# Two of the six selection blocks of a sparse-attention layer move from the attention heads into the indexer

## The chip, the core and the metric

The kernel runs on one core of a Trainium2 chip. The metric is the time of one execution on the device in microseconds (us), the median of three runs. The core has a matrix engine (PE, with weight loads as PEld), a vector engine (DVE), an activation engine (ACT), a general engine (POOL) and DMA queues fed by SP. Each engine takes its instructions strictly in the order of its own queue and waits at an instruction until the semaphores that it names are there.

## The reference, cut to what matters

The program is a decoder trunk of two layers (sequence 1024, width 1024). Layer 0 has two groups of softmax heads, layer 1 has eight stick-breaking heads and eight sparse heads, and each layer ends in a gated MLP with a short convolution. Only layer 1's attention is touched. Its sparse heads see, for each query, the 256 keys that an indexer scores highest:

```python
logits = jnp.einsum('bqhd,bkd->bqhk', iqb, ik)                 # 4 index heads of 64, one shared key
score = jnp.einsum('bqhk,bqh->bqk', jax.nn.relu(logits), iwb)  # weighted sum over the index heads
score = jnp.where(kpos[None, None, :] <= qpos[None, :, None], score, -jnp.inf)
_, sel = lax.top_k(score, top_k)                               # top_k = 256
```

```python
def stick_breaking_attention(q, k, v):
    z = einsum('bqhd,bkhd->bhqk', qb, k) * scale
    log1m = where(kpos < qpos, log_sigmoid(-z), 0)
    after = cumsum(log1m, reverse=True) - log1m
    a = where(kpos < qpos, exp(log_sigmoid(z) + after), 0)     # in the kernel: sigmoid, running product, multiply
    return einsum('bhqk,bkhd->bqhd', a, v)
```

## The kernel before, in words

Everything runs in fp32 as products of high and low halves: a product is three matmuls (`three`), and an operand is split by ACT (the high half) and DVE (the low half, L190). Queries go in eight blocks of 128. Block i sees 128 x (i+1) keys, so its score row is 128(i+1) wide. The order in each engine's queue is set by a scheduler from the order in which the program emits work, so emission acts as a priority; a PE instruction that is emitted early stands early in PE's queue.

The layer's attention has two stages.

**The index** (`index`, from L920). For each of eight token tiles of 128 it makes a key tile (a projection of 24 matmuls, 256 wide, in `proj_tok` with the weights `uk`; ACT's copy out at L929; a rotation on POOL, a norm) and a query tile (the same with `uq`). `keys(half)` transposes four key tiles (L913) and splits them; `scored(half, xs, b)` transposes the query tiles of one half for two index heads, and then for each block of that half and each head does the score matmuls (`psS<-kh,qs`), a relu on ACT (L978) and an update of the block's score tile `sc[i]` on DVE (L979). The two first blocks, 0 and 1, have at most 256 keys and need no selection, so `sc` exists for blocks 2 to 7. Before, the order is: key tiles 0 to 3, `keys(0)`, key tiles 4 to 7, query tiles (with `keys(1)` and the first scores among them), then the rest of the scores. Beside it runs `fill`, which takes units from a list of other projections (`between`): q and k of the first pair of heads (weights `w1t`), then 16 tiles of v (weights `w1v`).

Weights come through `wunit`: a raw load into `ra` (two buffers in all), a copy of the high half on ACT (`hx` for the index's weights, `ha` for the others, L200) and the low half on DVE (`lx`, `la`). `hx` and `lx` have two buffers each, just enough for `uk`, or for `uq`. A weight unit thus needs a free `ra`, and its copy needs a free `hx`.

**The heads.** Eight stick-breaking heads, then eight sparse heads. For each block a stick-breaking head does: scores on PE into `psS` (two buffers), two sigmoids on ACT (L758, L759), a running product on DVE (L761), a multiply on POOL (L763), transposes of the result and the product with v on PE, with copies on ACT (L355) and DVE (L190 `ptl`) between.

**The selection** (`topk`, L1003) finds, per query, the value of the 256th highest score by bisection over the 32 bits. It runs as a list of steps beside the heads: `next(todo)` after each block above 2, five per head. One round counts, for every block, how many scores reach the candidate: on DVE (L1025, one pass over the row with a sum) for the blocks in `by_dve`, on ACT (a Sign with a sum, L1032) for those in `by_act`; then DVE sets the next candidate for all blocks at once with three operations on a tile of 128 x 6 (L1051 `tkY`, L1052 `tkC`, L1047 `tkG`). The round's counts need the candidate, and the next candidate needs all counts. After 32 rounds come one count for each ACT block (greater than), and for each block a finishing of five passes on DVE (L1025, L1069, L1071, L1072, L1073) and one on POOL (L1074), which turn `sc[i]` into a mask. Before, `by_dve, by_act = [5, 6], [2, 3, 4, 7]`: all six blocks in one search. Its first round stands ahead of head 0, rounds 2 to 31 stand in heads 0 to 5, and round 32 with the finishing in heads 6 and 7. The sparse heads need the masks.

Of the kernel before, what the change touches and what calls it, by code (L numbers as in the profile page):

```python
# [10 lines left out]
F32 = mybir.dt.float32  # L11
# [3 lines left out]
I8 = mybir.dt.int8  # L15
U32 = mybir.dt.uint32
# [6 lines left out]
P = 128  # L23
D = 1024
S = 1024
NT = S // P
# [29 lines left out]
class Net:  # L56
# [660 lines left out]
    def odd_attn(self, h):  # L717
        nc, tc, A = self.nc, self.tc, self.A
        unit = partial(self.wunit, lo_eng="vector")
        with ExitStack() as st:  # L720
            ep = st.enter_context
            kv = ep(tc.tile_pool(name="kv", bufs=1))
            iw = kv.tile([P, NT, 4], F32, name="iw")
            sc = [None, None] + [kv.tile([P, P * (i + 1)], F32, name=f"sc{i}") for i in range(2, 5)]
# [164 lines left out]
            self.start(between())  # L889
            with tc.tile_pool(name="ix", bufs=1) as ix:  # L890
                due = 0.0
                for _ in self.index(h, ix, iw, sc, chd, cld, krd):
                    due += 0.2
                    self.fill(int(due))
                    due -= int(due)
            pp = ep(tc.tile_pool(name="pp", bufs=1))
            pt = ep(tc.tile_pool(name="pt", bufs=1))
            self.rounds = []
            todo = iter(self.topk(kv, pp, sc))
            while ("v", 0) not in self.ready:  # L900
                next(todo, None)
                self.fill(2)
# [13 lines left out]
    def index(self, h, ix, iw, sc, chd, cld, krd):  # L916

        nc, A = self.nc, self.A
# [4 lines left out]
        uk = [self.wunit(A["w1x"][1, u], [4, 256], ix, "x", lo_eng="vector") for u in range(2)]  # L923
# [13 lines left out]
        def query_tile(t):  # L937
            o = self.proj_tok(uq, h, t, 256)
            x = ix.tile([P, 320], F32, name="xt", tag="xt", bufs=8)[:, :256]
            nc.scalar.activation(x, o, AF.Copy)  # L940
            self.rope(x.rearrange("p (m d) -> p m d", d=HD), 4, t, ix)
            return x
# [38 lines left out]
                    yield  # L981


        xk, xq = [], []
        for t in range(NT):
            xk.append(key_tile(t))
            yield
            if t == 3:

                self.fill(4)  # L990
                yield from keys(0, xk)
        uq = [self.wunit(A["w1x"][0, u], [4, 256], ix, "x", lo_eng="vector") for u in range(2)]
        self.fill(2)
        for t in range(NT):
            xq.append(query_tile(t))
            yield
            if t == 1:
                yield from keys(1, xk[4:])
            if t == 5:
                yield from scored(0, xq[:4], 0)  # L1000
        yield from scored(0, xq[:4], 1)
        for b in range(2):
            yield from scored(1, xq[4:], b)  # L1003

    def topk(self, pool, jpool, sc):

        nc = self.nc
        by_dve, by_act = [5, 6], [2, 3, 4, 7]  # L1010
        blocks = by_dve + by_act
        k, kd = len(blocks), len(by_dve)

        T, M, C, G, Y = (pool.tile([P, k], U32, name=n) for n in ("tkT", "tkM", "tkC", "tkG", "tkY"))
        cnt, need = (pool.tile([P, k], F32, name=n) for n in ("cnt", "need"))
        Cf = C.bitcast(F32)
        nc.gpsimd.memset(Cf, 0.0)
        for j, i in enumerate(blocks):

            nc.gpsimd.memset(need[:, j:j + 1], float(TOPK if j < kd else 2 * TOPK - P * (i + 1)))  # L1020

        def count(x, t, out, op):
            n = x.shape[1]
            j = jpool.tile([P, S], I8, name="jv", tag="jv", bufs=1)
            return nc.vector.tensor_scalar(j[:, :n], x, t, 0.0, op0=op, op1=ALU.add, accum_out=out)  # L1025

        def counts():
            for j, i in enumerate(blocks):
                if j < kd:
                    d = count(sc[i], Cf[:, j:j + 1], cnt[:, j:j + 1], ALU.is_ge)  # L1030
                else:
                    a = nc.scalar.activation(self.junk[:, :P * (i + 1)], sc[i], AF.Sign, bias=Cf[:, j:j + 1], scale=1.0,  # L1032
                                             accum_out=cnt[:, j:j + 1])
            self.rounds.append((d, a))

        counts()
        yield

        nc.vector.tensor_tensor(Y, cnt, need, op=ALU.is_ge)
        nc.vector.tensor_scalar(T, Y, 31, None, op0=ALU.logical_shift_left)  # L1040
        nc.vector.tensor_scalar(M.bitcast(I32), T.bitcast(I32), 31, -1, op0=ALU.arith_shift_right, op1=ALU.bitwise_xor)
        nc.vector.tensor_scalar(M, M, 0x80000000, None, op0=ALU.bitwise_or)
        nc.vector.tensor_scalar(M[:, kd:], M[:, kd:], 0x80000000, None, op0=ALU.bitwise_xor)
        nc.vector.scalar_tensor_tensor(C, T, 1 << 30, M, op0=ALU.bitwise_or, op1=ALU.bitwise_xor)
        for b in range(30, -1, -1):
            if b:
                nc.vector.tensor_scalar(G, C, 1 << b - 1, None, op0=ALU.bitwise_xor)  # L1047
            counts()
            yield

            nc.vector.tensor_tensor(Y, cnt, need, op=ALU.is_lt)  # L1051
            nc.vector.scalar_tensor_tensor(C, Y, b, G if b else C, op0=ALU.logical_shift_left, op1=ALU.bitwise_xor)  # L1052
        nc.vector.tensor_tensor(T, C, M, op=ALU.bitwise_xor)

        nc.vector.tensor_scalar(M[:, kd:], M[:, kd:], 0x80000000, None, op0=ALU.bitwise_xor)
        nc.vector.tensor_tensor(C, T, M, op=ALU.bitwise_xor)
        for j in range(kd, k):
            count(sc[blocks[j]], Cf[:, j:j + 1], cnt[:, j:j + 1], ALU.is_gt)
        nc.vector.tensor_scalar(Y[:, kd:], cnt[:, kd:], float(TOPK), None, op0=ALU.is_ge)
        nc.gpsimd.tensor_tensor(T[:, kd:], T[:, kd:], Y[:, kd:], op=ALU.add)  # L1060
        nc.vector.tensor_tensor(C, T, M, op=ALU.bitwise_xor)
        yield
        for j, i in enumerate(blocks):
            n = P * (i + 1)
            v = Cf[:, j:j + 1]
            count(sc[i], v, cnt[:, j:j + 1], ALU.is_gt)
            nc.vector.tensor_scalar(cnt[:, j:j + 1], cnt[:, j:j + 1], -1.0, float(TOPK), op0=ALU.mult, op1=ALU.add)
            e = jpool.tile([P, S], I8, name="te", tag="jv", bufs=1)[:, :n]
            nc.vector.tensor_scalar(e, sc[i], v, 1.0, op0=ALU.is_equal, op1=ALU.mult)  # L1069
            r = self.Y("tr")[:, :n]  # L1070
            nc.vector.tensor_tensor_scan(r, self.ones[:, 0:1].to_broadcast([P, n]), e, 0.0, ALU.mult, ALU.add)  # L1071
            nc.vector.scalar_tensor_tensor(e, r, cnt[:, j:j + 1], e, op0=ALU.is_le, op1=ALU.mult)  # L1072
            nc.vector.scalar_tensor_tensor(sc[i], sc[i], v, e, op0=ALU.is_gt, op1=ALU.add)  # L1073
            nc.gpsimd.tensor_scalar(sc[i], sc[i], 1.0, -NEG, op0=ALU.subtract, op1=ALU.mult)  # L1074
            yield
# [452 lines left out]
```

## Time and profile before

| | us |
|---|---|
| median of three runs (lowest, highest) | 2750.49 (2749.03, 2751.11) |
| the profiled execution's own time | 2749.97 |
| its span, first to last instruction | 2748.1 |
| index, from the first key tile's matmul to head 0's first sigmoid | 1357.0 to 1498.6 |
| stick-breaking heads 0 to 7, from first sigmoid to first sigmoid | 1498.6, 1534.4, 1572.6, 1610.1, 1648.3, 1687.6, 1724.4, 1761.5 |
| first exponential of the sparse heads | 1813.0 |

All positions are microseconds from the start of the span. The two stages together last 456 us, a sixth of the span. In the whole span PE is busy 94%, DVE 70%, ACT 51% and POOL 29%; but these shares differ much from stage to stage, and the rows below are read by stage. "PEclk" is the clock granted to PE in a stretch as a share of its full speed; its two levels are 1.2 and 2.4 GHz, so 0.73 is a mix of both.

### The profile page before, as it was taken

How to read it: one execution, taken by the hardware profiler on the slowest of the kernel's cores; microseconds unless marked ns; L12 is line 12 of the kernel's file. 1: busy time of each engine (PE TensorE's matmuls, PEld its weight loads, DVE VectorE, ACT ScalarE, POOL GpSimd, SP SyncE). 2: the span in 40 equal slices, each digit the busy share in tenths (PEclk: the TensorE clock that was granted, in tenths of full speed). 3: DMA queues.
4: the chain of work that ended last, by engine and by line, in shares of the span. 5: the costliest groups of instructions: out<-in, count | busy, mean ns of one | idle time of the engine just before them, and what ended most of it. 6: DMA issues, size and time to landing. Idle time of an engine off the chain costs nothing. (4 is left out here: it accounts for less than half of the span.)

```text
span 2748.1 us, 38746 instructions
## 1 busy us (share of the span) xinstructions
PE 2589.5 (94%) x14088; PEld 2175.3 (79%) x14088; DVE 1918.5 (70%) x2783; ACT 1399.1 (51%) x2432; POOL 788.9 (29%) x1036
## 2 busy tenths in 40 slices
PE   7999999889999999999999999679998999999998
PEld 6878889778788888777888788457796888887876
DVE  4554555735788887777536898988647888887676
ACT  4454544523544444444435899658525444444443
POOL 0243534522333333000131334344405333331000
PEclk9999999989999999999999899789999999999999
DMA  6342322432133323564331333325522332324733
GB/s 117 118 112 62 97 68 70 120 111 81 62 119 104 119 82 130 187 207 119 123 91 41 76 83 115 95 55 152 171 77 77 104 109 87 115 100 168 250 104 115
DMA packets 148816, 301.71 MB, mean 110 GB/s; under 512 B 40137, under 2 KB 43337, under 8 KB 148497
## 3 DMA queue, kind: packets, MB, share of 16 engines
q1 hardware_dynamic: 148624, 299.24, 36.1%
q8 instruction: 111, 1.82, 0.3%
q14 instruction: 81, 0.66, 0.1%
HBM read 185.63 MB, written 74.22 MB: 95 GB/s over the span
## 5 line engine op out<-in xcount | busy, mean ns | idle before, releaser
L190 DVE TENSOR_TENSOR ptl<-psB,pth 128x512 fp32r<-128x512 f32 x280 | 181.9, 658 | 93.2 <-ACT pth L355 88.0
L84 PE MATMUL psB<-ha,hh 128*128 128x256 f32 (+1 forms) x768 | 222.0, 290 | 2.7 <-DVE v L190 1.9
L84 PE MATMUL psB<-la,hh 128*128 128x256 f32 (+1 forms) x768 | 218.0, 284 | 0.0
L84 PE MATMUL psB<-ha,hl 128*128 128x256 f32 (+1 forms) x768 | 217.7, 284 | 0.0
L211 POOL TENSOR_TENSOR rs<-rs,mhalf 128x1 f32<-128x1 f32 x48 | 32.3, 678 | 641.8 <-DVE rs L210 641.6
L84 PE MATMUL psS<-kh,qs 128*128 128x512 f32 (+2 forms) x424 | 168.4, 398 | 43.9 <-DVE t L761 31.4
L355 ACT ACTIVATE pth<-psB 128x512 fp32r<-128x512 f32 x280 | 158.5, 576 | 79.4 <-PE psB L349 61.0
L349 PE MATMUL psB<-identf,p 128*128 128x128 f32 x1008 | 176.1, 284 | 21.6 <-DVE p L644 9.2
L190 DVE TENSOR_TENSOR la<-ra,ha 128x1024 fp32r<-128x1024 f32 (+1 forms) x92 | 118.4, 1287 | 107.2 <-ACT ha L1186 67.4
L84 PE MATMUL psS<-la,ah 128*128 128x512 f32 x432 | 171.4, 397 | 6.5 <-DVE la L190 6.5
L84 PE MATMUL psS<-ha,al 128*128 128x512 f32 x432 | 169.6, 393 | 0.0
L349 PEld LDWEIGHTS psB<-identf,p 128*128 128x128 f32 x1008 | 128.2, 146 | 44.3 <-DVE p L644 9.8
L1186 ACT ACTIVATE ha<-ra 128x1024 fp32r<-128x1024 f32 x44 | 46.6, 1060 | 221.0 <-DMA ra<-in_wi_dram 206.5
L84 PE MATMUL psS<-ha,ah 128*128 128x512 f32 x432 | 155.0, 396 | 4.1 <-DVE x L1348 3.9
L84 PE MATMUL psO<-pth,v 128*128 128x512 f32 (+2 forms) x384 | 149.7, 397 | 9.2 <-ACT pth L355 4.8
L84 PE MATMUL psS<-kl,qs 128*128 128x512 f32 (+2 forms) x424 | 149.9, 360 | 2.7 <-DMA kl<-kl 2.6
L1234 POOL TENSOR_TENSOR sr<-rb 128x512 f32<-128x512 f32 x44 | 59.0, 1340 | 322.5 <-issue 283.2
L84 PEld LDWEIGHTS psB<-ha,hh 128*128 128x128 f32 x768 | 146.9, 192 | 5.1 <-DVE v L190 2.1
L84 PEld LDWEIGHTS psB<-la,hh 128*128 128x128 f32 x768 | 146.7, 191 | 1.2 <-DVE la L190 0.2
L84 PEld LDWEIGHTS psB<-ha,hl 128*128 128x128 f32 x768 | 146.3, 191 | 0.4
L763 POOL TENSOR_TENSOR p<-p,t 128x127 f32<-128x127 f32 (+3 forms) x64 | 83.1, 1299 | 207.0 <-DVE t L761 203.6
L84 PEld LDWEIGHTS psS<-kh,qs 128*128 128x128 f32 x424 | 83.0, 196 | 67.5 <-DVE t L761 36.4
(368 smaller groups left out, 8250.1 us busy)
## 6 DMA issues: line engine op xcount, KB each, us to landing
ra<-in_wi_dram SPq DMA_DIRECT2D x44, 512.0 KB, 3.9
rb<-in_wi_dram SPq DMA_DIRECT2D x44, 512.0 KB, 3.5
ar<-act SPq DMA_DIRECT2D x78, 256.0 KB, 2.7
ra<-act SPq DMA_DIRECT2D x76, 256.0 KB, 2.7
kh<-kh SPq DMA_DIRECT2D x96, 128.0 KB, 2.3
kl<-kl SPq DMA_DIRECT2D x96, 128.0 KB, 2.4
ot<-oa SPq DMA_DIRECT2D x96, 128.0 KB, 2.4
ro<-ot SPq DMA_DIRECT2D x24, 512.0 KB, 3.9
```

The source lines that it names most:

```text
L84: self.nc.tensor.matmul(out, lhsT, rhs, start=start, stop=stop, skip_group_check=True)
L190: return getattr(self.nc, eng).tensor_tensor(dst, src, hi.bitcast(F32), op=ALU.subtract)
L211: nc.gpsimd.tensor_tensor(rs, rs, self.mhalf[:, 0:1], op=ALU.pow)
L349: nc.tensor.transpose(t[:, c:c + P], H.pr[q][:, j * P:(j + 1) * P], self.identf)
L355: nc.scalar.activation(hi[:, :used], t[:, :used], AF.Copy)
L763: nc.gpsimd.tensor_tensor(p[:, :n - 1], p[:, :n - 1], t1[:, 1:n], op=ALU.mult)
L1186: self.nc.scalar.activation(hi, raw, AF.Copy)
L1234: nc.gpsimd.tensor_tensor(s12[:, 0:4], rv[:, 0:4], rv[:, 4:8], op=ALU.add)
```

## The change

The index is written in another order. It takes the first 512 tokens whole: key tiles 0 to 3 with `uk`, the loads of `uq`, four units of fill, `keys(0)`, query tiles 0 to 3, and both scorings of blocks 2 and 3. Then it takes query tiles 4 to 7, loads `uk` a second time (its buffers have held `uq` since), and takes key tiles 4 to 7, `keys(1)` and the scores of blocks 4 to 7. `topk` becomes a function of its blocks. A first search over blocks 3 (counted on DVE) and 2 (counted on ACT) is stepped once at each step of the index, 30 steps, and drained at its end, so that it and its finishing are emitted ahead of the heads. The second search, over block 7 on DVE and blocks 4, 5 and 6 on ACT, runs beside the heads as the whole search did. The number of units of fill taken in the index is about as before.

```diff
-                for _ in self.index(h, ix, iw, sc, chd, cld, krd):
-                    due += 0.2
+                self.rounds = []
+                early = self.topk(ix, ix, sc, [3], [2])
+                for _ in self.index(h, ix, iw, sc, chd, cld, krd):
+                    next(early, None)
+                    due += 0.25
                     self.fill(int(due))
                     due -= int(due)
+                for n, _ in enumerate(early):
+                    self.fill(n % 2)
...
-            todo = iter(self.topk(kv, pp, sc))
+            todo = iter(self.topk(kv, pp, sc, [7], [4, 5, 6]))
...
-        xk, xq = [], []
-        for t in range(NT):
+        xk = [key_tile(t) for t in range(4)]
+        uq = [self.wunit(A["w1x"][0, u], [4, 256], ix, "x", lo_eng="vector") for u in range(2)]
+        self.fill(4)
+        for _ in keys(0, xk):
+            pass
+        xq = [query_tile(t) for t in range(4)]
+        h[1]
+        for b in range(2):
+            for _ in scored(0, xq, b):
+                pass
+        yield
+        xq = []
+        for t in range(4, NT):
+            xq.append(query_tile(t))
+            yield
+        uk = [self.wunit(A["w1x"][1, u], [4, 256], ix, "x", lo_eng="vector") for u in range(2)]
+        self.fill(2)
+        xk = []
+        for t in range(4, NT):
             xk.append(key_tile(t))
             yield
-            if t == 3:
-
-                self.fill(4)
-                yield from keys(0, xk)
-        uq = [self.wunit(A["w1x"][0, u], [4, 256], ix, "x", lo_eng="vector") for u in range(2)]
-        self.fill(2)
-        for t in range(NT):
-            xq.append(query_tile(t))
-            yield
-            if t == 1:
-                yield from keys(1, xk[4:])
-            if t == 5:
-                yield from scored(0, xq[:4], 0)
-        yield from scored(0, xq[:4], 1)
+        self.fill(1)
+        yield from keys(1, xk)
         for b in range(2):
-            yield from scored(1, xq[4:], b)
+            yield from scored(1, xq, b)
 
-    def topk(self, pool, jpool, sc):
+    def topk(self, pool, jpool, sc, by_dve, by_act):
...
-        by_dve, by_act = [5, 6], [2, 3, 4, 7]
         blocks = by_dve + by_act
         k, kd = len(blocks), len(by_dve)
```

What it does to the queues is seen at three places. The first is SP's queue at the start of the index, where `w1x` are the index's weights, `w1t` those of q and k of the first pair of heads, and `xd` the layer's input put aside. Before:

```order
L197 DMA ra<-in_w1x_dram 128x1024 x2
L1430 DMA xd<-x 128x1024 x4
L197 DMA ra<-in_w1t_dram 128x1024 x2
L197 DMA ra<-in_w1x_dram 128x1024 x2
L274 DMA qs<-qs 64x512
```

After:

```order
L197 DMA ra<-in_w1x_dram 128x1024 x2
L1440 DMA xd<-x 128x1024 x4
L197 DMA ra<-in_w1x_dram 128x1024 x2
L197 DMA ra<-in_w1t_dram 128x1024 x2
L197 DMA ra<-in_w1x_dram 128x1024 x2
L274 DMA qs<-qs 64x512
```

The query weights now stand ahead of `w1t`, and the key weights come a second time behind it. The second place is ACT's queue in the same stretch: `hx` is the high half of the index's weights, `ha` that of `w1t`, `xt` the copy of a finished key tile. Before:

```order
L200 ACTIVATE hx<-ra 128x1024 x2
L200 ACTIVATE ha<-ra 128x1024 x2
L929 ACTIVATE xt<-psB 128x256
L208 ACTIVATE junk,ss<-xt 128x128
```

After:

```order
L200 ACTIVATE hx<-ra 128x1024
L934 ACTIVATE xt<-psB 128x256
L200 ACTIVATE hx<-ra 128x1024
L208 ACTIVATE junk,ss<-xt 128x128
L208 ACTIVATE junk,ss<-x 128x1024 x2
L200 ACTIVATE ha<-ra 128x1024
L208 ACTIVATE junk,ss<-x 128x1024
L200 ACTIVATE ha<-ra 128x1024
```

The rows of after begin behind the third key tile's copy: the copies of `w1t` stand behind those of the query weights, which stand around the fourth key tile. PE's own queue has the same sequence in both: four key tiles, then the 48 matmuls of `w1t`. The third place is DVE's queue at the end of the index, where `sc_1293x` are the score tiles (0 is block 2, 5 is block 7), `t` the running product of head 0 and `v` the low halves of the values. Before:

```order
L979 SCALAR_TENSOR_TENSOR sc_12933<-rl,iw,sc_12933 128x768 x2
L190 TENSOR_TENSOR v<-psB,v 128x4x64
L1025 TENSOR_SCALAR jv,cnt<-sc_12933,tkC 128x768
L979 SCALAR_TENSOR_TENSOR sc_12934<-rl,iw,sc_12934 128x896 x2
L979 SCALAR_TENSOR_TENSOR sc_12935<-rl,iw,sc_12935 128x1024
L1025 TENSOR_SCALAR jv,cnt<-sc_12934,tkC 128x896
L979 SCALAR_TENSOR_TENSOR sc_12935<-rl,iw,sc_12935 128x1024
L761 SCALAR_TENSOR_TENSOR t_14450<-psS,zeros 128x128
```

After, where some 200 rows stand between the first count of the early search and head 0's first running product; they begin

```order
L1035 TENSOR_SCALAR jv,cnt_13561<-sc_12931,tkC_13558 128x512
L1061 TENSOR_TENSOR tkY_13560<-cnt_13561,need_13562 128x2
L210 TENSOR_SCALAR rs<-ss 128x1
L1062 SCALAR_TENSOR_TENSOR tkC_13558<-tkY_13560,tkG_13559 128x2
L1057 TENSOR_SCALAR tkG_13559<-tkC_13558 128x2
L1035 TENSOR_SCALAR jv,cnt_13561<-sc_12931,tkC_13558 128x512
L939 TENSOR_SCALAR xt<-xt,rs 128x128
```

with round upon round of this kind, and end

```order
L1035 TENSOR_SCALAR jv,cnt_13561<-sc_12930,tkC_13558 128x384
L1077 TENSOR_SCALAR cnt_13561<-cnt_13561 128x1
L1079 TENSOR_SCALAR te<-sc_12930,tkC_13558 128x384
L1081 SCALAR_TENSOR_TENSOR tr<-ones,te 128x384
L1082 SCALAR_TENSOR_TENSOR te<-tr,cnt_13561,te 128x384
L1083 SCALAR_TENSOR_TENSOR sc_12930<-sc_12930,tkC_13558,te 128x384
L1035 TENSOR_SCALAR jv,cnt_14605<-sc_12935,tkC_14602 128x1024
L761 SCALAR_TENSOR_TENSOR t_14689<-psS,zeros 128x128
```

Those rows hold 32 counts of 512 with their small operations, the end of the early search, the finishing of blocks 3 and 2 (the row of L1083 is the last of it), the first count of block 7, 16 updates of blocks 4 to 7 and 15 low halves of v.

## Rows read from the trace of the kernel before

**Rows 1.** Busy time by stretch: length; PE, PEld, DVE, ACT, POOL; clock; DMA share, rate.

```profile
1357.00:1400.00 43.00, 41.42 (x258) 35.98 (x257) 17.70 (x35) 19.34 (x40) 14.98 (x50) 0.96 0.37 102
1400.00:1498.60 98.60, 96.85 (x737) 92.64 (x735) 42.92 (x63) 41.75 (x78) 23.05 (x82) 1.00 0.24 64
1498.60:1534.40 35.80, 27.68 (x131) 22.44 (x132) 28.99 (x49) 29.34 (x60) 8.38 (x8) 0.86 0.22 56
1534.40:1687.60 153.20, 147.56 (x922) 127.39 (x921) 136.05 (x228) 143.18 (x303) 65.22 (x129) 0.97 0.30 76
1687.60:1724.40 36.80, 33.13 (x168) 26.70 (x169) 33.00 (x62) 34.48 (x75) 11.10 (x11) 0.97 0.57 166
1724.40:1813.00 88.60, 55.30 (x240) 37.66 (x238) 82.40 (x123) 47.90 (x92) 34.91 (x22) 0.73 0.35 88
```

**Rows 2.** PE's waits from 1550 to 1700: us in total, times, longest.

```profile
PE psS L84 <- DVE t L761: 2.0, 4, 0.7
```

**Rows 3.** The same view from 1700 to 1830.

```profile
PE psS L84 <- DVE t L761: 20.6, 12, 6.2
```

**Rows 4.** Timeline of PE where key tile 3 ends: start, duration, instruction.

```profile
1368.93 0.28 PE L84 MATMUL psB<-hx,hl 128*128 128x256 f32 x1
1369.05 0.40 PE L84 MATMUL psB<-hh,ha 128*128 128x512 f32 x1
```

**Rows 5.** Timeline of SP's queue there; the second number is the issue's own time.

```profile
1356.39 1.47 SPq L197 DMA_DIRECT2D ra<-in_w1t_dram  x2
```

**Rows 6.** Timeline of ACT there; in brackets the idle time before and its releaser.

```profile
1361.49 1.06 ACT L200 ACTIVATE ha<-ra 128x1024 fp32r<-128x1024 f32 x1 [5.46 <-DMA ra<-in_w1t_dram]
```

**Rows 7.** Timeline of DVE there.

```profile
1362.58 2.49 DVE L190 TENSOR_TENSOR la<-ra,ha 128x1024 fp32r<-128x1024 f32 x2 [5.08 <-ACT ha L200]
```

**Rows 8.** Timeline of DVE at head 0's first running product.

```profile
1499.53 1.00 DVE L761 TENSOR_TENSOR_SCAN t<-psS,zeros 128x128 f32<-128x128 f32 x2
```

**Rows 9.** Timeline of DVE for one round of the search in head 5.

```profile
1716.60 0.21 DVE L1051 TENSOR_TENSOR tkY<-cnt,need 128x6 uint32<-128x6 f32 x1 [0.43 <-ACT junk L1032]
1716.84 0.17 DVE L1052 SCALAR_TENSOR_TENSOR tkC<-tkY,tkG 128x6 uint32<-128x6 uint32 x1
1717.04 0.70 DVE L1047 TENSOR_SCALAR tkG<-tkC 128x6 uint32<-128x6 uint32 x1
1717.12 1.00 DVE L1025 TENSOR_SCALAR_CACHE_REDUCE jv<-sc,tkC 128x768 int8<-128x768 f32 x1
...
1719.24 2.28 DVE L761 TENSOR_TENSOR_SCAN t<-psS,zeros 128x1024 f32<-128x1024 f32 x1
```

**Rows 10.** DVE's groups by shape, 1440 to 1816: count, busy us, mean ns, idle before.

```profile
L190 DVE TENSOR_TENSOR v<-psB,v 128x256 fp32r<-128x256 f32 x21 | 8.8, 419 | 8.8 <-ACT v L503 8.7
L979 DVE SCALAR_TENSOR_TENSOR sc<-rl,iw,sc 128x1024 f32<-128x1024 f32 x4 | 5.1, 1280 | 2.1 <-ACT rl L978 2.1
...
L979 DVE SCALAR_TENSOR_TENSOR sc<-rl,iw,sc 128x640 f32<-128x640 f32 x4 | 3.5, 882 | 2.1 <-ACT rl L978 1.9
...
L1025 DVE TENSOR_SCALAR_CACHE_REDUCE jv<-sc,tkC 128x1024 int8<-128x1024 f32 x2 | 2.5, 1267 | 0.0
...
L1025 DVE TENSOR_SCALAR_CACHE_REDUCE jv<-sc,tkC 128x512 int8<-128x512 f32 x2 | 1.5, 734 | 0.0
...
L1071 DVE TENSOR_TENSOR_SCAN tr<-ones,te 128x512 f32<-128x512 f32 x1 | 1.2, 1209 | 0.0
```

**Rows 11.** ACT's groups by shape in the same stretch.

```profile
L1032 ACT ACTIVATE junk<-sc,tkC 128x1024 int8<-128x1024 f32 x32 | 36.8, 1150 | 0.6
...
L1032 ACT ACTIVATE junk<-sc,tkC 128x384 int8<-128x384 f32 x32 | 19.6, 614 | 3.7 <-DVE tkC L1052 1.5 <-DVE sc L979 1.0 <-DVE tkC L1044 1.0
```

**Rows 12.** Timeline of DVE in head 7: three of the five passes that finish block 3.

```profile
1787.71 0.70 DVE L1069 TENSOR_SCALAR te<-sc,tkC 128x512 int8<-128x512 f32 x1
...
1791.91 0.72 DVE L1072 SCALAR_TENSOR_TENSOR te<-tr,cnt,te 128x512 int8<-128x512 f32 x1
...
1793.62 0.74 DVE L1073 SCALAR_TENSOR_TENSOR sc<-sc,tkC,te 128x512 f32<-128x512 f32 x1
```

More of the change, by code (lines that the diff above doesn't have):

```diff
@@ L981, in scored @@
                     yield
-        xk, xq = [], []
-        for t in range(NT):
+        xk = [key_tile(t) for t in range(4)]
[17 more added lines that the diff above has]
+        for t in range(4, NT):
             xk.append(key_tile(t))
             yield
-            if t == 3:
-                self.fill(4)
-                yield from keys(0, xk)
-        uq = [self.wunit(A["w1x"][0, u], [4, 256], ix, "x", lo_eng="vector") for u in range(2)]
-        self.fill(2)
-        for t in range(NT):
-            xq.append(query_tile(t))
-            yield
-            if t == 1:
-                yield from keys(1, xk[4:])
-            if t == 5:
-                yield from scored(0, xq[:4], 0)
-        yield from scored(0, xq[:4], 1)
+        self.fill(1)
+        yield from keys(1, xk)
         for b in range(2):
-            yield from scored(1, xq[4:], b)
-    def topk(self, pool, jpool, sc):
+            yield from scored(1, xq, b)
+    def topk(self, pool, jpool, sc, by_dve, by_act):
         nc = self.nc
-        by_dve, by_act = [5, 6], [2, 3, 4, 7]
         blocks = by_dve + by_act
         k, kd = len(blocks), len(by_dve)
-        T, M, C, G, Y = (pool.tile([P, k], U32, name=n) for n in ("tkT", "tkM", "tkC", "tkG", "tkY"))
-        cnt, need = (pool.tile([P, k], F32, name=n) for n in ("cnt", "need"))
+        T, M, C, G, Y = (pool.tile([P, k], U32, name=f"{n}{k}") for n in ("tkT", "tkM", "tkC", "tkG", "tkY"))
+        cnt, need = (pool.tile([P, k], F32, name=f"{n}{k}") for n in ("cnt", "need"))
+        width = P * (max(blocks) + 1)
         Cf = C.bitcast(F32)
@@ L1023, in count @@
             n = x.shape[1]
-            j = jpool.tile([P, S], I8, name="jv", tag="jv", bufs=1)
+            j = jpool.tile([P, width], I8, name="jv", tag="jv", bufs=1)
             return nc.vector.tensor_scalar(j[:, :n], x, t, 0.0, op0=op, op1=ALU.add, accum_out=out)
@@ L1067, in topk @@
             nc.vector.tensor_scalar(cnt[:, j:j + 1], cnt[:, j:j + 1], -1.0, float(TOPK), op0=ALU.mult, op1=ALU.add)
-            e = jpool.tile([P, S], I8, name="te", tag="jv", bufs=1)[:, :n]
+            e = jpool.tile([P, width], I8, name="te", tag="jv", bufs=1)[:, :n]
             nc.vector.tensor_scalar(e, sc[i], v, 1.0, op0=ALU.is_equal, op1=ALU.mult)
```

## The prediction, made before the changed kernel ran

> **What bounds the kernel now.** I read the busy time by stretch first [rows 1], then PE's waits in the heads [rows 2, 3], then the timelines at the places where queues change [rows 4 to 9]. Three regimes are to be seen. In the index (1400 to 1498.6) PE is busy 96.85 of 98.6 us, DVE 42.9 and ACT 41.8: PE sets the pace and DVE has 56 us to spare. In heads 1 to 4 (153.2 us) PE is busy 147.6, ACT 143.2, DVE 136.1: the three are almost in balance, and PE, the last of them, leaves only 5.6 us; over most of that stretch PE waited 2.0 us for the running product [rows 2]. In heads 6 and 7 (88.6 us) DVE is busy 82.4 and PE 55.3: DVE, with the finishing of six blocks on it, is the bound, and PE waited 20.6 us for the running product [rows 3]. Heads 0 and 5 lie between (PE idle 8.1 and 3.7 us). So work taken off DVE pays in full in heads 6 and 7, in part in heads 0 and 5, and by a few us in heads 1 to 4; work put on DVE in the index is free until DVE's spare time is used up.
>
> **The change, part by part.** *Index start.* PE runs from key tile 3 into the projection with `w1t` with no gap (1368.93, 1369.05) [rows 4]. It can, because `w1t` was issued at 1356.39 and copied from 1361.49 [rows 5, 6], while key tiles ran. After, `w1t` stands behind `uq` in `ra`, whose copies need `hx`, which key tile 3 still reads. A key tile is 24 matmuls at 0.12 apart, 2.8 us, so the first `hx` is free at about 1367.8. Then one copy (1.06) and one low half (1.25, half of 2.49 [rows 7]) free `ra` at 1370.3; from issue to copy took 5.1 us before, so `w1t` is there at 1375.4; the copy (1.06) and low half follow and PE goes on at about 1377.3. PE's queue has the same sequence as before, so nothing fills the gap: **+8 us** at this place. Bounds: 0 if the loads come sooner than I place them, +10 if the second unit is late too.
>
> *The early search.* By the matmuls of the first half (about 59 us of PE work from 1357, plus the 8, plus some 2 for transposes) blocks 2 and 3 have their last scores near 1426; the evacuations, relu and updates behind them take some 7 us, so the first count starts near 1433. From there to head 0's first running product DVE must do, in its queue's order: 32 rounds; each is a candidate step of three operations 0.2 us apart [rows 9], whose width of 2 or 6 makes no difference to me, and a count of 512 (0.73 and a reading 0.08, less overlap) [rows 10], together 1.2, so 38.7; the end of the search with its two counts 2.9; the finishing of block 3, 0.73 + 0.70 + 1.21 + 0.72 + 0.74 = 4.1 [rows 10, 12], and of block 2, three quarters as wide, 3.0; the first count of block 7, 1.2; 16 updates between 0.88 and 1.28, 17.3 [rows 10]; 15 low halves of v at 0.33 net of overlap (0.42 each alone [rows 10]), 5; norms, splits and weights 8.3. That is 81 us. ACT's part of a round, a Sign of 384 (0.61 [rows 11] and a reading), fits beside DVE's 1.2 when ACT is free; where it is behind a relu or a copy the round waits, for which I add 4. So the first running product comes at 1433 + 85 = 1518, where it was at 1499.5 [rows 8]: **+19**, and DVE, not PE, is the bound at the index's end. The 8 us of the PE gap are inside this, since they set when the search can begin. PE is not late there: three tiles of v move behind head 0's first score, each 24 matmuls at 0.12, 8.7 us in all, which pays for the gap; so PE stands at head 0 about when it did and waits for DVE some 19 us. Bounds: +14 with no gap at the start and no waits; +30 if ACT holds up each round by 0.35 us more (11 us).
>
> Here the Trainium skill speaks against the change: "VectorE: DVE Perf Modes", section "The TRN2 errata", says that an operation on SBUF pays a fixed cost per instruction, so that many small tiles pay it many times. Splitting one search into two doubles the small operations. The row agrees: 0.17 us for six columns [rows 9]. Were their cost in proportion to width, the early rounds would be 32 times 0.4 = 12.8 us cheaper and the first product at 1505; by the rule it is as in the sum.
>
> *Heads.* A round's counts on DVE were 1717.12 to 1719.24, 2.12 us [rows 9]; now one count of 1024 at 1.27 [rows 10], 1.24 net: -0.88 a round, 4.4 a head. On ACT the four Signs (384, 512, 640, 1024) are 3.31 by the rows of 384 and 1024 [rows 11] with the widths between on the line through them; the three now (640, 768, 896) 2.81, and one reading less: -0.55 a round, 2.75 a head. Head 0, where PE is idle 8.1 us and its scores now wait ready: -3.5. Heads 1 to 4: PE's idle 5.6 us is all that can be had, and a little of the slow clock (0.97): -7. Head 5: -3. Heads 6 and 7, bound by DVE: the finishing of blocks 2 and 3 is gone (7.1), two late rounds are lighter (1.8), and three counts of ACT blocks in place of four (0.4): -9.5. The sum of the unrounded terms is **-23.5**. Bounds: -15 if heads 1 to 4 give nothing and the tail shares its gain with POOL's multiplies and PE's slow clock (0.73 there); -33 if DVE's and ACT's savings come through in heads 0 to 5 at some 4 us each.
>
> *Free.* The second load of `uk` (two DMAs of 512 KB, two copies, two low halves) lies under query tiles 4 to 7; the two low halves are in the 8.3 above. If it is late, PE waits once more, but PE has those 19 us in hand, so that costs nothing until it delays the updates.
>
> *Sum.* +19 - 23.5 = -4.5 against the profiled execution's 2749.97: 2745.5. That execution is 0.5 under the median, so I say **2746**.
>
> **Rivals.** *The rounds hide* (faster). The early search begins sooner, near 1425, since the gap at the start is short, and waits of DVE in the index are few: the first product comes at +8, the heads give 24: -16, **2734**. For it: DVE has 56 us idle in the index [rows 1] and the added work is 47 us. Against: that idle time lies mostly ahead of 1433, where no score of blocks 2 and 3 is ready. It decides if the first count starts before 1426.
>
> *The search's own loop is late* (slower). In each round DVE waits for ACT's Sign, ACT in its queue stands behind a relu that waits for PE, and PE waits for a score tile that ACT frees; DVE meanwhile can't go on to the next update. Such waits exist before (0.43 us ahead of the candidate in rows 9). At 0.5 us more on 32 rounds the first product comes at +34; heads 1 to 4 are PE's and give little, so the heads give 20 to 24: +10 to +14, **2761**. It decides if a round takes over 1.6 us where the updates are few.
>
> *PE is the true bound in the heads* (no change). Heads 0 to 5 give 6 in all, the tail 9.5, the index costs 15: 0, **2750**. This lies within my forecast's range and shares its chance.
>
> *It does not do what it says*: the scheduler could leave the early rounds till the heads. DVE's queue rules that out: all 32 counts and both finishings stand ahead of the first running product.
>
> **How the numbers follow.** Forecast with its neighbours (2738 to 2753): 0.5. Rounds hide: 0.25. Late loop: 0.25. The range must leave out 2 in 10: it reaches through most of both, 2731 to 2761. 0.2% is 5.5 us, about what a measurement of this kernel can tell from no change: faster means below 2745, slower above 2756. The forecast at 2746 lies just inside, so its half divides into 0.18 faster, 0.30 same, 0.02 slower; the hidden rounds give 0.24 and 0.01; the late loop 0.03 same and 0.22 slower. Faster 0.42, same 0.34, slower 0.24.
>
> **What would show it.** Right: PE idle about 8 us behind key tile 3; the first count of 512 near 1433; DVE busy over 90% from there to a first running product near 1518; the heads' first sigmoids closer together by 1 to 4 us; heads 6 and 7 shorter by 9 to 10. Wrong: no gap behind key tile 3; rounds of over 1.6 us with DVE idle in them; heads 1 to 4 as long as before, or shorter by 3 or more each.

## The result, and the profile after

The changed kernel takes **2777.99 us** (median of four runs, 2772.57 to 2783.03) where the kernel before took 2749.76 beside it: a ratio of 1.0104, with a 95% interval of 1.0081 to 1.0126. Forecast were 2746 and a range of 2731 to 2761. It is slower by 28 us; the slow side had been given 0.24.

The profiled execution is the longest of the four (span 2781.2), and its index begins 5.7 us later than in the trace of before (the loads of the index's weights are issued at 1344.80 instead of 1339.11), though nothing in the program up to there was changed. So stages are compared by their lengths. Busy time by stretch (length; PE, PEld, DVE, ACT, POOL; clock), as [rows 1]:

```profile
1362.70:1405.70 43.00, 34.49 (x216) 30.39 (x215) 13.72 (x26) 15.14 (x31) 16.75 (x53) 0.88 0.39 117
1405.70:1529.40 123.70, 107.82 (x779) 100.44 (x778) 92.06 (x255) 68.97 (x152) 26.39 (x83) 0.96 0.21 54
1529.40:1561.40 32.00, 25.94 (x116) 20.58 (x117) 25.46 (x39) 25.43 (x48) 9.13 (x9) 0.76 0.15 43
1561.40:1720.40 159.00, 146.22 (x911) 125.71 (x910) 126.13 (x185) 132.75 (x264) 63.24 (x125) 0.97 0.29 74
1720.40:1766.40 46.00, 41.60 (x207) 34.04 (x206) 35.32 (x59) 34.18 (x70) 12.75 (x16) 0.93 0.61 167
1766.40:1845.60 79.20, 50.71 (x226) 36.15 (x224) 72.66 (x100) 44.35 (x85) 31.48 (x20) 0.76 0.29 74
```

| stage, us | before | after | difference | forecast |
|---|---|---|---|---|
| index, to head 0's first sigmoid | 141.6 | 166.7 | +25.1 | +19 |
| head 0 | 35.8 | 32.0 | -3.8 | -3.5 |
| heads 1 to 4 | 153.2 | 159.0 | +5.8 | -7 |
| head 5 | 36.8 | 46.0 | +9.2 | -3 |
| heads 6 and 7 | 88.6 | 79.2 | -9.4 | -9.5 |

By their lengths the two ends of the heads did what was forecast. The index cost 6 us more than forecast, and heads 1 to 5, with less work on DVE and ACT than before, took 15 us more instead of 10 less. Within them heads 1 and 2 fell by 3.8 together, and heads 3, 4 and 5 rose from 38.2, 39.3 and 36.8 us to 42.3, 44.8 and 46.0. Single heads are not quite comparable: PE's other work moved between them. The rows show 207 matmuls in head 5 where [rows 1] has 168, and 226 in heads 6 and 7 where it has 240, so a part of head 5's rise is work that came from elsewhere. Heads 0 to 7 together hold nearly as many as before (1460 and 1461), and took 1.8 us more.

At the index's start the gap is there. PE behind key tile 3 (timeline; in brackets the idle time before and its releaser), and SP's queue ahead of it:

```profile
1379.00 0.80 PE L84 MATMUL psB<-hh,ha 128*128 128x512 f32 x1 [5.62 <-ACT ha L200]
1382.06 0.80 PE L84 MATMUL psB<-hh,la 128*128 128x512 f32 x1 [1.83 <-DVE la L190]
```

```profile
1362.09 1.47 SPq L197 DMA_DIRECT2D ra<-in_w1x_dram  x2
1374.35 2.08 SPq L197 DMA_DIRECT2D ra<-in_w1t_dram  x2
```

`w1t` goes out 12.3 us after the query weights, since its `ra` is held till their copies find `hx` free; PE stands 5.6 and 1.8 us, 7.4 in all. Before it ran through [rows 4].

DVE in the early search: the first count, two rounds of it, and head 0's first running product:

```profile
1440.77 0.74 DVE L1035 TENSOR_SCALAR_CACHE_REDUCE jv<-sc,tkC 128x512 int8<-128x512 f32 x1
...
1443.66 0.16 DVE L1061 TENSOR_TENSOR tkY<-cnt,need 128x2 uint32<-128x2 f32 x1
1443.86 0.16 DVE L1062 SCALAR_TENSOR_TENSOR tkC<-tkY,tkG 128x2 uint32<-128x2 uint32 x1
1444.06 0.17 DVE L1057 TENSOR_SCALAR tkG<-tkC 128x2 uint32<-128x2 uint32 x1
1444.14 0.74 DVE L1035 TENSOR_SCALAR_CACHE_REDUCE jv<-sc,tkC 128x512 int8<-128x512 f32 x1
...
1444.99 0.22 DVE L1061 TENSOR_TENSOR tkY<-cnt,need 128x2 uint32<-128x2 f32 x1
...
1529.86 0.42 DVE L761 TENSOR_TENSOR_SCAN t<-psS,zeros 128x128 f32<-128x128 f32 x1 [0.52 <-ACT psS L759]
```

A round takes 1.33 us (1443.66 to 1444.99) where nothing comes between. From the first count to the first running product it is 89.1 us; 85 were forecast. The first count is 96.0 us behind the issue of the index's weights, 2.1 later than forecast (1433 less 1339.1).

In heads 3 to 5 a wait has appeared. Waits of ACT (total us, times, longest), first of the kernel before from 1610.1 to 1724.4, then of the changed kernel from 1633.3 to 1766.4, then DVE's of the changed kernel there:

```profile
ACT junk L1032 <- DVE tkC L1052: 0.9, 2, 0.6
```

```profile
ACT junk L1042 <- DVE tkC L1062: 17.6, 10, 2.6
```

```profile
DVE ptl L190 <- ACT pth L355: 16.9, 11, 3.5
DVE t L761 <- ACT psS L759: 10.0, 7, 3.3
```

ACT waits at a round's first Sign for DVE's candidate `tkC`, and DVE in its turn waits for ACT's copies and sigmoids. One such place in head 4, ACT, then DVE, then POOL:

```profile
1697.05 0.71 ACT L758 ACTIVATE p<-psS 128x640 f32<-128x640 f32 x1
1697.65 0.70 ACT L759 ACTIVATE psS<-psS 128x640 f32<-128x640 f32 x1
1698.27 0.60 ACT L355 ACTIVATE pth<-psB 128x512 fp32r<-128x512 f32 x1
1701.44 0.83 ACT L1042 ACTIVATE junk<-sc,tkC 128x640 int8<-128x640 f32 x1 [2.58 <-DVE tkC L1062]
...
1702.54 0.80 ACT L758 ACTIVATE p<-psS 128x768 f32<-128x768 f32 x1
```

```profile
1698.45 1.49 DVE L761 TENSOR_TENSOR_SCAN t<-psS,zeros 128x640 f32<-128x640 f32 x1 [0.65 <-ACT psS L759]
1699.86 0.14 DVE L1061 TENSOR_TENSOR tkY<-cnt,need 128x4 uint32<-128x4 f32 x1
1699.91 0.69 DVE L190 TENSOR_TENSOR ptl<-psB,pth 128x512 fp32r<-128x512 f32 x1
1700.51 0.84 DVE L1062 SCALAR_TENSOR_TENSOR tkC<-tkY,tkG 128x4 uint32<-128x4 uint32 x1
```

```profile
1700.02 1.31 POOL L763 TENSOR_TENSOR p<-p,t 128x639 f32<-128x639 f32 x1 [1.98 <-DVE tkY L1061]
```

The order of the two queues closes a loop. On DVE a round's candidate stands behind the running product of the block just done (that is written so in the program, before and after). On ACT the Signs that need this candidate stand right behind that block's own sigmoids, with no other sigmoid between: so ACT, but for one copy, has nothing to do from its sigmoids till DVE has made product and candidate, and stands 2.58 us. If the *next* block's sigmoids stand ahead of the Signs, ACT works meanwhile. The program allows both, since a sigmoid only has to stand behind the Signs of the round but one (`behind(1, 2)`); the scheduler chooses. In heads 3 to 5, 1 of 15 rounds stood bare in this way before (its first Sign ahead of the next block's sigmoids), and 7 of 15 do now. The bare rounds hold 11.1 of the 17.6 us; the other waits are at rounds whose Signs do stand behind the next sigmoids, but whose candidate came late all the same. Why the scheduler chose otherwise for the lighter rounds wasn't looked for.

### The profile page after: what moved, and what is told of

Same layout as the page of the kernel before. It is cut to its first block, busy times and chain, and to the rows that moved or that the text cites. A ratio compares the mean times of both kernels' runs of the same rounds, so it can differ in the third digit from the quotient of the medians.

```text
span 2781.2 us, 38882 instructions
## 1 busy us (share of the span) xinstructions
PE 2597.0 (93%) x14088; PEld 2181.1 (78%) x14088; DVE 1942.9 (70%) x2888; ACT 1403.7 (50%) x2434; POOL 791.3 (28%) x1038
## 3 DMA queue, kind: packets, MB, share of 16 engines
q1 hardware_dynamic: 148912, 300.29, 35.8%
## 5 line engine op out<-in xcount | busy, mean ns | idle before, releaser
L84 PE MATMUL psB<-ha,hh 128*128 128x256 f32 (+1 forms) x768 | 224.4, 293 | 7.2 <-DVE v L190 2.9
L84 PE MATMUL psO<-ptl,v 128*128 128x512 f32 x336 | 129.3, 391 | 4.7 <-DVE ptl L190 4.0
```

The source lines that it names most:

```text
L84: self.nc.tensor.matmul(out, lhsT, rhs, start=start, stop=stop, skip_group_check=True)
```

## Experiments

Four theories were told apart. **A**: PE sets the pace in heads 0 to 5, and three tiles of v, 8.7 us of PE work that the prediction let slide behind head 0's first score, are paid there. **B**: three wide Signs in a row make the round's loop longer. **C**: DVE's backlog at the index's end spoils the heads. **D** (formed after the first four runs): the order on ACT.

**e1_fill_in_index**

```diff
-                    due += 0.25
+                    due += 0.35
```

> The changed kernel (2778.0) with three more units of fill in the index (0.35 a step instead of 0.25), so that PE's queue has the same fill ahead of head 0 as the kernel before had: 470 us of PE work instead of 461. Theory A (PE sets the pace of heads 0 to 5, and the three tiles of v that slid behind head 0's first score, 8.7 us of PE work, are paid there, while PE idles in the index): head 0's first sigmoid later by 0 to 2, heads 0 to 5 shorter by 8 to 11, in all 2768 to 2771. Theory B (the heads lose because three wide Signs in a row on ACT make the search's loop longer): heads 3 to 5 stay at 42 to 46 us each, in all 2777 to 2780.

Measured: 2775.29 us, ratio 1.0086 (1.0069 to 1.0104), not to be told from the changed kernel's 1.0104. In its trace heads 0 to 5 take 235.5 us (237.0 in the changed kernel). Theory A's 8 to 11 us aren't there. By itself this is a weak test, since ACT's waits for the candidate in these heads grew as well (27.1 us, 22.3 in the changed kernel). But the traces take away the theory's ground: in the changed kernel one tile of v is copied out behind head 0's first sigmoid (at 1543.08), and one was before (at 1510.43). The tiles that slid behind head 0's first score (1510.08) ran right behind it, and then PE still waited 10.5 us for DVE.

**e2_w1t_first**

```diff
         xk = [key_tile(t) for t in range(4)]
+        self.fill(4)
         uq = [self.wunit(A["w1x"][0, u], [4, 256], ix, "x", lo_eng="vector") for u in range(2)]
-        self.fill(4)
```

> The changed kernel with one exchange: the four units of fill, and with them the loads of w1t, are emitted ahead of the loads of the query weights. The gap of PE behind key tile 3 (5.6 + 1.8 us in the changed kernel's trace) goes. If the early search is a chain on DVE that starts when blocks 2 and 3 are scored, the first count and head 0's first sigmoid both come 7 us earlier: 2771. If DVE waits in that stretch for PE's later scores instead, the first sigmoid moves by under 3: 2775 to 2778.

Measured: 2768.98 us, ratio 1.0062 (1.0047 to 1.0077). PE has no gap behind key tile 3 any more, and the first count and the first running product move together:

```profile
1427.30 0.74 DVE L1035 TENSOR_SCALAR_CACHE_REDUCE jv<-sc,tkC 128x512 int8<-128x512 f32 x1
...
1514.93 0.42 DVE L761 TENSOR_TENSOR_SCAN t<-psS,zeros 128x128 f32<-128x128 f32 x1 [0.52 <-ACT psS L759]
```

They are 87.6 us apart, as in the changed kernel (89.1), and against the issue of the index's weights (1340.95 here) they come 9.6 and 11.1 us earlier. So the index's end is a chain that starts when blocks 2 and 3 are scored, and the gap of 7.4 us at the start is paid in full and somewhat more. The whole program gains 9.0 us; in this trace heads 0 to 5 take 242.1 us, 5 more than in the changed kernel, with 25.2 us of ACT's waits for the candidate (21.3 there).

**e3_no_early**

```diff
-                early = self.topk(ix, ix, sc, [3], [2])
+                early = iter(())
```

> The changed kernel without the early search (blocks 2 and 3 are left unselected, so the sparse heads see more keys there); order of the index, gap and the search of four blocks beside the heads stay. It prices the early search. Index from 166.7 back to 141 to 145 us. Theory A: three tiles of v still stand in the heads, so heads 0 to 5 stay at 233 to 238 us: 2753 to 2756. Theory C (the heads start badly because DVE is 20 us behind at their beginning): heads 0 to 5 fall by 8 or more: 2742 to 2746.

Measured: 2756.43 us, ratio 1.0018 (1.0008 to 1.0028). The early search costs the difference, 0.0086 of 2750, some 24 us. In the trace the index takes 147.8 us (166.7 with the search), and heads 0 to 5 still take 238.7. They do hold some PE work more (1272 matmuls, 1230 in the changed kernel), but that is 4.5 us of PE's busy time and can't hide the 8 us of theory C. The wait for the candidate is there as in the changed kernel, 23.6 us. So the heads are slow without any backlog: theory C falls.

**e4_light_heads**

```diff
-        by_dve, by_act = [5, 6], [2, 3, 4, 7]
+        by_dve, by_act = [7], [4, 5, 6]
```

> The kernel before (2749.8) with blocks 2 and 3 left out of the search (unselected), block 7 counted on DVE and 4, 5, 6 on ACT, as beside the heads of the changed kernel; the index as before. It prices what the lighter search gives in the heads by itself. The prediction's term: -23.5, so 2726. Theory A (PE sets the pace of heads 0 to 5): -9.5 from heads 6 and 7 and 0 to -4 from the rest: 2736 to 2740. Theory B (the new division of blocks makes the loop longer): heads 3 to 5 longer by 13, so 2752 to 2755.

Measured: 2759.21 us, ratio 1.0033 (1.0018 to 1.0047). This was the run that decided: the kernel before, with two blocks' counts and finishing simply left out, gets *slower*. Its index takes 141.8 us, its heads 0 to 2 107.6 (before 111.5), and heads 3 to 5 take 43.9, 44.8 and 47.8: the loss of the changed kernel without its index. ACT's wait is there too (1496.4 to 1740.5):

```profile
ACT junk L1032 <- DVE tkC L1052: 26.0, 17, 2.6
```

By its sign theory B had said this, with 13 us in heads 3 to 5 where 22 were measured; but a round has less on ACT now (2.8 us of Signs in place of 3.3 by the rows of the prediction), and ACT is not busy but waiting. That gave theory D, which the next four runs test with the work left as it is and only the order changed. The first three move a whole round's steps, DVE's as well as ACT's, behind the next block's sigmoids; e8 changes nothing but where ACT's sigmoids may stand.

**e5_after_sig_ahead**, on the changed kernel; **e6_light_sig_ahead**, the same edit on e4_light_heads; **e7_before_sig_ahead**, on the kernel before:

```diff
-                    with self.behind(1, 2):
+                    with self.behind(1, 1 if held else 2):
                         nc.scalar.activation(p, s, AF.Sigmoid)
-                    nc.scalar.activation(s, s, AF.Sigmoid, scale=-1.0)
+                    sig = nc.scalar.activation(s, s, AF.Sigmoid, scale=-1.0)
+                    if held:
+                        with tc.issue_after(held.pop().ins), tc.issue_after(sig.ins):
+                            next(todo, None)
...
                     if i > 2:
-                        with tc.issue_after(scan.ins):
-                            next(todo, None)
+                        held.append(scan)
```

**e8_before_sig_behind**, on the kernel before, forces the other order:

```diff
-                    with self.behind(1, 2):
+                    with self.behind(1, 1):
```

> The changed kernel (2778.0) with another order on ACT alone: a round's three Signs stand behind the next block's two sigmoids in every round, where now two of five stand ahead of them in heads 3 to 5. Theory D (in those rounds ACT waits at the Sign for a candidate that DVE makes behind the running product of the block just done, while DVE waits for the next sigmoids, which stand behind the Signs: 17.6 us of ACT's waits in heads 3 to 5): these waits fall under 4 us, heads 3 to 5 from 133 to 115 to 121 us, in all 2760 to 2766. Theory A (PE's extra tiles of v): no change, 2775 to 2780.

> The kernel before with blocks 2 and 3 left out of the search (unselected), as in e4_light_heads (2759.2), and the sigmoids ahead of the Signs in every round. Theory D: the lighter search gives what it should, heads 3 to 5 from 136 to 113 to 116 us and the tail's 9.5: 2736 to 2742. The prediction's term of -23.5 would show as 2726 to 2728. Theory A: as e4_light_heads, 2757 to 2761.

> The kernel before with the sigmoids ahead of the Signs in every round; it has them so in four of five rounds already. Theory D: 0 to -5, 2745 to 2751. If the forced order costs something by itself (Signs later, so candidates later): 2752 to 2758.

> The kernel before, same work, with the other order forced: each block's sigmoids behind the last round's Signs, so that every one of the 30 rounds in heads 0 to 5 has the wait. Theory D: some 26 rounds more with about 2 us each, of which PE's fill can cover a part: 2780 to 2805, ACT's waits for the candidate 40 us or more. If the order doesn't matter: 2748 to 2755.

| kernel | us | ratio to before (95%) | ACT's wait for the candidate, about heads 0 to 5, us |
|---|---|---|---|
| after | 2777.99 | 1.0104 (1.0081 to 1.0126) | 21.3 |
| e5_after_sig_ahead | 2762.56 | 1.0046 (1.0030 to 1.0061) | 3.1 |
| e4_light_heads | 2759.21 | 1.0033 (1.0018 to 1.0047) | 26.0 |
| e6_light_sig_ahead | 2740.98 | 0.9963 (0.9948 to 0.9978) | 2.8 |
| e7_before_sig_ahead | 2754.43 | 1.0011 (1.0000 to 1.0021) | 0.7 |
| e8_before_sig_behind | 2826.65 | 1.0278 (1.0256 to 1.0300) | 67.8 |

The kernel before has 1.5 us of this wait. ACT's waits in e5, e6 and e8, one row each:

```profile
ACT junk L1046 <- DVE tkC L1066: 3.1, 4, 1.0
```

```profile
ACT junk L1036 <- DVE tkC L1056: 2.8, 4, 1.0
```

```profile
ACT junk L1032 <- DVE tkC L1052: 67.8, 28, 6.1
```

Theory D holds on both sides, and theory B falls with e6: the same three wide Signs a round, without the wait, are 18 us faster. Mended, the changed kernel wins 15 us and the light kernel 18; in e5 heads 0 to 5 take 224.4 us instead of 237.0. Spoiled, the kernel before loses 75 us with the same work, more than expected; its six heads take 303.6 us where they took 225.8. A part of that came through PE's clock: for nearly the same number of matmuls (1218 before, 1238 in e8) PE is busy 228.4 us in these heads instead of 208.4, at a mean granted clock of 0.85 instead of 0.95, a mix of its two levels. On the kernel before, which had the good order nearly everywhere, the edit gains nothing (0 to -5 were expected), and may cost 0 to 0.2%. Heads 3 to 5 missed their forecasts: 123.3 us in e5 (115 to 121 expected) and 123.4 in e6 (113 to 116), with 45.3 us in head 5 alone, which holds 203 matmuls there and 168 before.

e6 also prices the term of the prediction. With the order out of the way the lighter heads give 11 us against the kernel before (13 against e7), where 23.5 were forecast, and in its trace heads 0 to 5 still take 228.0 us (225.8 before, 224.4 in e5); what is gained shows in heads 6 and 7. Heads 0 to 7 together take 303.1 us in e6 and 300.3 in e5, where the kernel before took 314.4. Heads 0 to 5, before and then e6:

```profile
1498.60:1724.40 225.80, 208.37 (x1218) 176.53 (x1219) 198.03 (x338) 207.00 (x435) 84.70 (x147) 0.95 0.33 88
```

```profile
1505.30:1733.30 228.00, 210.93 (x1234) 178.28 (x1234) 182.83 (x285) 193.61 (x380) 83.38 (x147) 0.94 0.35 93
```

**e12_no_search**

```diff
-            todo = iter(self.topk(kv, pp, sc))
+            todo = iter(())
```

> The kernel before with no selection at all (all blocks unselected, so the sparse heads see every earlier key): neither rounds nor finishing beside the heads, 11 us less on DVE and 18.4 less on ACT in every head. It asks what the heads can give at most. If PE bounds heads 0 to 5 (92% busy there before), they stay at 210 to 225 us, and heads 6 and 7 fall from 87 to 55 to 62: 2700 to 2722. If DVE and ACT bound them, heads 0 to 5 fall in proportion to ACT's 18.4 us a head, to 170 or less: 2650 to 2675.

Measured: 2684.74 us, ratio 0.9756 (0.9732 to 0.9779), between the two expectations. By stage (e12's head 0, head 1, heads 2 to 5, and heads 6 and 7; then heads 2 to 5 of the kernel before):

```profile
1498.11:1518.62 20.51, 18.02 (x96) 14.58 (x96) 16.46 (x15) 13.45 (x23) 8.43 (x8) 0.92 0.16 52
1518.62:1550.31 31.69, 30.98 (x171) 25.48 (x170) 18.76 (x23) 18.44 (x34) 8.86 (x8) 1.00 0.39 90
1550.31:1696.20 145.89, 145.89 (x954) 129.17 (x952) 81.33 (x92) 79.28 (x145) 65.06 (x131) 1.00 0.40 107
1696.20:1743.50 47.30, 38.77 (x225) 28.56 (x223) 40.07 (x51) 37.93 (x72) 21.79 (x17) 1.00 0.54 134
```

```profile
1572.60:1724.40 151.80, 144.47 (x900) 124.26 (x899) 135.26 (x232) 143.02 (x304) 63.18 (x125) 0.99 0.35 96
```

In heads 2 to 5 PE is busy in the whole of 145.89 us at full clock, with DVE and ACT little over half busy: that is PE's floor there. By its length it is only 5.9 us under the time before, but it holds 954 matmuls where these heads held 900: fill moved into them from heads 0 and 1 and from the tail. So heads 0 to 5 are better taken whole. They take 198.1 us instead of 225.8, 27.7 less, with as many matmuls (1216 and 1218); PE's idle time falls from 17.4 to 3.2 us, and its busy time by 13.5 us (208.4 to 194.9), at a mean granted clock of 0.99 instead of 0.95. Heads 6 and 7 fall by 40. Neither expectation was right for the whole: without the search heads 1 to 5 are PE's, but heads 0 to 5 had 28 us to give, more than was expected of a bound by PE.

**e9_both** joins the edits of e2 and e5. **e10_tail_beside** then moves the end of the early search out of the index (its steps after the 24th go into the heads behind the running products of blocks 1 and 2; its small tiles are packed in two, and both searches share one scratch row). **e11_swap_2_3** is e9 with `topk(ix, ix, sc, [2], [3])`. The core of e10's edit:

```diff
-                early = self.topk(ix, ix, sc, [3], [2])
-                for _ in self.index(h, ix, iw, sc, chd, cld, krd):
-                    next(early, None)
+                early = self.topk(kv, kv, sc, [3], [2], False)
+                for s, _ in enumerate(self.index(h, ix, iw, sc, chd, cld, krd)):
+                    if s < 24:
+                        next(early, None)
...
-                for n, _ in enumerate(early):
-                    self.fill(n % 2)
+                self.fill(2)
...
                     if i > 2:
                         held.append(scan)
+                    elif i:
+                        with tc.issue_after(scan.ins):
+                            next(early, None)
```

> The changed kernel with both mendings: w1t's loads ahead of the query weights (as e2, -9.0 by itself) and the sigmoids ahead of the Signs (as e5, -15.4 by itself). If the two losses are independent, one at the index's start and one in the heads, they add: 2778.0 - 24.4 = 2753 to 2756, 2 to 5 above the kernel before, which is then the cost of the early search that the lighter heads don't give back. If one hides the other (a DVE that is early at head 0 only waits there), 2759 to 2763.

> e9_both, but the early search takes only 24 steps in the index; its last 11 steps (some 8 rounds, the end of the search, the finishing of blocks 3 and 2; about 20 us of DVE's queue) go beside heads 0 to 5, after blocks 1 and 2. If DVE's queue is what holds head 0 back at the index's end, the first sigmoid comes 10 to 14 us earlier (PE is ready for head 0 some 15 us ahead of DVE), and the heads, bound by PE, take the steps for 3 to 8: 2745 to 2750. If the heads are bound by DVE and ACT, they give it all back: 2753 to 2758.

> e9_both with the two early blocks exchanged: block 2 (384 wide) counted on DVE, block 3 (512) on ACT. DVE's 32 counts get 0.12 us shorter each (0.73 to 0.61), ACT's Signs 0.11 longer. If DVE's queue sets the index's end: -3 to -4, 2750 to 2752. If the round's loop through ACT sets it: +1 to +4, 2755 to 2759.

Measured: e9 2750.83 us, ratio 1.0005 (0.9994 to 1.0015); e10 **2740.19 us, ratio 0.9966 (0.9952 to 0.9979)**; e11 2749.75, ratio 1.0002 (0.9991 to 1.0012). The two losses add, to 27 us: mended, the change is as fast as the kernel before. With the tail of the search beside the heads it is faster than both kernels, by 0.3% against the kernel before. Its first running product and its heads 0 to 5, then those of e9:

```profile
1499.55 0.42 DVE L766 TENSOR_TENSOR_SCAN t<-psS,zeros 128x128 f32<-128x128 f32 x1
```

```profile
1499.07:1730.70 231.63, 213.20 (x1298) 181.09 (x1296) 204.88 (x350) 199.02 (x398) 88.19 (x150) 0.99 0.34 91
```

```profile
1512.91:1738.37 225.46, 207.87 (x1234) 175.95 (x1234) 181.93 (x283) 192.89 (x380) 83.87 (x148) 0.96 0.36 94
```

The index takes 138.6 us (156.9 in e9), 18 less, and heads 0 to 5 231.6 (225.5 in e9), 6 more: most of the work that held DVE up at the index's end costs nothing beside the heads. These heads take 64 matmuls more as well, three tiles of v among them, since the edit also takes fewer units of fill ahead of head 0; PE's busy time rises by 5.3 us only, at a mean granted clock of 0.99 instead of 0.96. e11 settles nothing: 1 us lies inside both intervals, so whether DVE's counts or the loop through ACT is the tighter in the early search stays open. How much of e10's gain is the 11 moved steps, and how much the moved fill, wasn't tried either.

## Why the prediction was wrong

**The step that failed is "Heads", the term of -23.5.** It summed less work, and took the order of the queues from before. Measured in the profile, heads 0 to 7 together gave +1.8 us. (Its parts don't quite add up, 23.0 as written and 9.3 in the tail, but that is half a us.) Two things were wrong in it:

- *The order.* 15 of the 25 us between -23.5 and +1.8 are this (2778.0 to 2762.6 by e5; in the traces heads 0 to 7 fall from 316.2 to 300.3). The prediction did look at the queues, at three places, but only at the index and at the start of the heads; the one place where ACT's queue changed inside the heads, Signs ahead of the next sigmoids, wasn't among them, though both queues could have been read there. "Heads 1 to 4 are PE's" fitted the kernel before, where PE waited 2.0 us for the running product [rows 2]; it doesn't follow that lighter work on the other engines can't lengthen them.
- *The size.* Without the loss of order the lighter heads give 11 to 13 us, not 23.5. Of the 13.5 claimed for heads 0 to 5, next to nothing came: 224.4 us in e5 and 228.0 in e6, against 225.8. It isn't so that nothing was to be had there, since the whole search costs these heads 27.7 us (e12); why two of its six blocks brought nothing stays open. Nor is PE's idle time [rows 1], by which the prediction sized heads 1 to 4, the limit: in heads 0 to 5 it is 17.4 us, and e12 gains more, since PE's busy time falls as well. Heads 6 and 7 gave 9.4 for 9.5 in the changed kernel and 12.7 in e5, but that they came so near is in part luck, since some of their work had moved into head 5 (heads 6 and 7 hold 240 matmuls before, 226 in the changed kernel, 213 in e5).

**The index term** had the right mechanism, mis-sized by 6 of 25: forecast +19, measured +25.1. The early search started 2.1 us later than forecast and its chain took 4.1 us longer. The gap (+8 forecast, 7.4 measured) and DVE's chain (85 forecast, 89.1 measured) are as described; that DVE, not PE, ends the index is shown by e2, where count and product move together, and by e3, where the index is 19 us shorter without the search. DVE isn't over 90% busy there, though: the waits were 14 us and not 4, the longest 2.9 us for one copy by ACT. The small operations cost the same for 2 columns (0.16 us) as for 6 (0.17) [rows 9], and the sum was right to keep them whole; the Trainium skill's fixed cost per instruction ("VectorE: DVE Perf Modes", section "The TRN2 errata") agrees with it.

**The rivals.** "The search's own loop is late" had the right engines, ACT's Sign and DVE's candidate in a circle, and ended on the right side; but it was placed in the index, where a round took 1.33 us and DVE waited 0.2 us in all for a Sign, and not in the heads, where the circle was. "PE is the true bound in the heads" was right that heads 0 to 5 would give little; but PE fills heads 2 to 5 only once the whole search is gone (e12), so the reason it gave isn't shown. That the lighter heads could get longer wasn't among the cases, and so the range ended 17 us short.

## What to carry to other kernels

When a change lightens a round of work on engines that feed each other, read the order of both queues again at every place where they meet, not only where the diff is: Signs that stood ahead of the next sigmoids on ACT made waits of 0.6 to 2.6 us each in heads 3 to 5, cost 15 us in all, and 75 us where the order was forced everywhere. If such an order matters, write it into the program rather than leave it to a scheduler's estimate. What lighter work on two engines can give at most is read from a run with that work left out, and not from the third engine's idle time: here that was 17 us, and the run without the search gained 28. And compare stages only with the work that stands in them: count their matmuls first.

## What the runs showed of the hardware

The candidate's tiny operation (L1052 before, two inputs of 4 or 6 columns) isn't always tiny. DVE's groups by shape in heads 1 to 5, for the kernel before, the changed one, e5 and e8 (count, busy us, mean ns):

```profile
L1052 DVE SCALAR_TENSOR_TENSOR tkC<-tkY,tkG 128x6 uint32<-128x6 uint32 x25 | 6.5, 261 | 0.8
```

```profile
L1062 DVE SCALAR_TENSOR_TENSOR tkC<-tkY,tkG 128x4 uint32<-128x4 uint32 x25 | 13.9, 556 | 0.7
```

```profile
L1066 DVE SCALAR_TENSOR_TENSOR tkC<-tkY,tkG 128x4 uint32<-128x4 uint32 x24 | 7.7, 320 | 0.8
```

```profile
L1052 DVE SCALAR_TENSOR_TENSOR tkC<-tkY,tkG 128x6 uint32<-128x6 uint32 x25 | 27.2, 1088 | 0.4
```

Alone it takes 0.17 us [rows 9]. In the bad order it comes right behind a running product, just after POOL has started to multiply with that product, and ends when POOL does: 1700.51 + 0.84 is 1701.35, and POOL's multiply ends at 1701.33. In heads 0 to 5 of before, after, e5, e6 and e8 there are 141 such instructions: 52 took more than 0.3 us, and each of these ended within 0.03 us of a multiply of POOL's; the other 89 took 0.18 at most. The Trainium skill, "SBUF — State Buffer", section "Who interferes with whom", says that a DVE instruction with two inputs in SBUF shares a port with GpSimd's reads as an exclusive lock, and that the one issued first decides who waits; the trace agrees. It makes the loop dearer: of the 2.58 us of ACT's wait above, 0.67 is this lock, and in e8 it is 0.9 us of a round on average.
